# Shifting the weight buffers of an fp32 encoder kernel by steps of 64 bytes in SBUF, and a smaller reserve for DMA descriptors

## The chip, the cores and the metric

The kernel runs on one NeuronCore of a Trainium2 chip (trn2). The metric is the device time of one execution in microseconds; three executions of the kernel before the change are at hand, and one further execution was recorded by the hardware profiler.

A NeuronCore has five engines that run side by side and meet only at semaphores. TensorE (PE) multiplies matrices: a weight load brings a stationary operand of 128 columns into the array, and a matmul then streams a moving operand past it and adds into PSUM. VectorE (DVE) and ScalarE (ACT) work elementwise, GpSimd (POOL) is nearly unused here, and SyncE (SP) issues the DMAs. The on-chip memory SBUF has 128 partitions; a tile of 4 KB here means 4 KB in every partition.

## The reference, cut to what matters

The program is two layers of an encoder on 512 tokens with a model width of 1,024, all in float32.

```
for l in range(DEPTH):                                     # DEPTH = 2
    mod = (cond @ w_ada[l] + b_ada[l])                     # six vectors of 1024
    h = _rmsnorm(x, norm1_w[l]) * (1.0 + sc1) + sh1
    x = x + g1 * _token_mixers(h, w_in[l], ..., w_out[l])  # conv, dilated attention, HGRN2
    h = _rmsnorm(x, norm2_w[l]) * (1.0 + sc2) + sh2
    x = x + g2 * _conv_ffn(h, w_up[l], conv_f_w[l], w_down[l])
return _rmsnorm(x, final_norm_w)
```

The large products are `h @ w_in` (1,024 to 3,584 columns), the mixed heads times `w_out` (1,024 to 1,024), `h @ w_up` (1,024 to 5,632) and the gated result times `w_down` (2,816 to 1,024). Between the first two lie three token mixers; between the last two lies a depthwise convolution of width 3 with a gelu gate.

## The kernel before, in words

**Products in three passes.** TensorE multiplies here in the type fp32r. Because one such product does not carry all the bits of a float32, every operand is held as two parts: a high part, which is the value cast to fp32r, and a low part, which is what the cast left over. A product is then the sum of three: high by high, high weight by low activation, low weight by high activation. The method `block` (lines 399 to 412) issues the three for one 128 by 128 piece of a weight:

```
        self.mm(ps, wh[:, s], ah, first if start is None else start, False)
...
        self.mm(ps, wh[:, s], al, False, False)
...
        self.mm(ps, wl[:, s], ah, False, last)
```

Of three matmuls two load their stationary operand from the high part `wh` of the weight and one from the low part `wl`. `s` is a slice of 128 columns, thus 512 bytes, so every slice of a buffer starts at the same place within 512 bytes as the buffer does. The moving operand is 512 tokens wide in the loop `tile_gemm` (line 712) and 256 wide in `first_group` and `last_group` (lines 683 and 618), which work on halves of the tokens at the seams between the stages.

**The way of a weight.** The weights are cut into chunks of up to 1,024 columns, in the order of their use (`run`, lines 1339 to 1358). `loader` (line 351) issues one DMA on SP for each chunk, into one of three buffers `wr`. `splitter` (line 358) makes the parts: a cast on ACT or DVE writes `wh` from `wr`, and a subtraction on DVE writes `wl` from `wr` and `wh`. There are four buffers `wh0` to `wh3` and four `wl0` to `wl3`, taken in turn: `sb` (line 225) takes the free buffer of a tag that was freed longest ago. Chunks that are marked wide (those of `first_group` and `last_group`) may also use buffers of other tags as weights: `qk`, `PT`, `KK`, `QQ`, `S`, `TT`, `bias`, `wa` and `ap`.

**What sets the order.** The kernel is written as generators. `run_threads` (line 322) advances them by priority and by a model of the engines' clocks (the class `Clock`, line 110) while the program is built, and the order of the instructions on every engine is the order in which they were issued then. The model knows the sizes of the tiles and the costs of operations; it does not look at addresses.

**Where the buffers lie.** `place` (line 218) takes all SBUF buffers once, in the order of the list `ORDER`, before any other tile, so that they lie one behind the other. The list `BUFFERS` gives the size of each in KB and their number:

```
BUFFERS = dict(wr=(4, 3), wh=(4, 4), wl=(4, 4), hx=(4, 8), qk=(4, 2), PT=(4, 4), KK=(4, 1), QQ=(4, 1), S=(4, 1),
               TT=(6, 1), ao=(2, 2), vr=(2, 2), va=(2, 1), bias=(4, 2), wa=(4, 1), tmp=(2, 5), P=(2, 2), sc=(1, 1),
               ap=(4.25, 1), acc=(2, 2), sm=(0.03125, 8), km=(2, 1), gs=(2, 3), qr=(2, 2), t2=(2, 2))
ORDER = ["wh", "wl", "wa", "bias", "wr", "tmp", "km", "P", "ap", "acc", "gs", "qr", "vr", "va", "ao", "t2", "sc",
         "hx", "PT", "TT", "qk", "KK", "QQ", "S", "sm"]
```

The sizes of the buffers ahead of `ap`, and of those from `acc` to `S`, are multiples of 512 bytes; `ap` with 4,352 bytes is eight and a half times 512. So all of `wh`, `wl`, `wa`, `bias`, `wr`, `tmp`, `km`, `P` and `ap` start at the same place within 512 bytes, and all of `acc` to `S`, with the activations `hx` among them, start 256 bytes off that place. Counted in lines of 64 bytes, of which eight make 512, the two groups are four lines apart. Ahead of all of them lies a stretch of SBUF that is reserved for descriptors of DMAs whose descriptors software writes; the keyword `dynamic_dma_scratch_size` of the program's constructor in `kernel` (line 1423) sets its size.

Of the kernel before, what the change touches and what calls it, by code (L numbers as in the profile page):

```python
# [9 lines left out]
F32 = mybir.dt.float32  # L10
# [182 lines left out]
class Kernel:  # L193
# [23 lines left out]

    def place(self):

        for tag in ORDER:  # L220
            for o in self.free_slots[tag]:
                self.one.tile([128, o["size"]], F32, tag=o["name"], name=o["name"] + "_0")


# [1212 lines left out]
```

## Time and profile before

| what | value |
|---|---|
| median of three runs | 1370.9 us (1370.58 to 1371.35) |
| the profiled execution's own time | 1370.76 us |
| its span, first to last instruction | 1369.0 us |
| mean granted clock of TensorE | 0.991 |
| instructions | 24,502 |
| bytes moved by DMA | 169.19 MB, mean 124 GB/s |

The profile records one execution. Its span is 1.76 us shorter than the time of that execution, which also holds what lies before the first and after the last instruction. "PE" are matmuls and "PEld" weight loads, which run ahead of the matmuls and overlap them. A line such as L274 is the line in the code that issues the instruction; L274 is the helper for matmuls and L181 the helper for all operations of DVE and ACT, so groups are told apart by the names of the tiles, output first, then inputs. Buffer numbers are left out of the names. A matmul's recorded duration holds its latency; how fast matmuls follow each other has to be read from their starts.

### The profile page before, as it was taken

The numbers are of one execution on the slowest core, as the hardware profiler recorded it, in microseconds if no ns is written. First come the engines' busy times: TensorE is split into PE (matmuls) and PEld (weight loads), VectorE is DVE, ScalarE is ACT, GpSimd is POOL, SyncE is SP. The second block draws the span as 40 slices with busy tenths as digits, with TensorE's granted clock in tenths as the row PEclk, the third lists the DMA queues.
The fourth block names the chain that finished last, engine by engine and source line by source line (L and its number), as shares of the span: only waits on it lengthen the run. The fifth ranks groups of instructions, "written<-read, shape, count | busy, mean of one in ns | idle before, by whom it ended". The sixth has DMA issues, their size and how long they took to land.

```text
span 1369.0 us, 24502 instructions
## 1 busy us (share of the span) xinstructions
PE 1344.9 (98%) x10042; PEld 1112.4 (81%) x10042; DVE 1070.0 (78%) x1841; ACT 609.6 (45%) x1017; POOL 2.1 (0%) x16
## 2 busy tenths in 40 slices
PE   8999999999999999999999999999999999999997
PEld 7977767778988888888899777777898888888887
DVE  6799999898599999766695999888868565556666
ACT  4537556565342433333453473746535232233332
POOL 0000000000000000000000000000000000000000
PEclk8999999999999999999999999999999999999998
DMA  9534443232348788432431312011422323323221
GB/s 353 189 134 142 124 151 94 81 105 89 103 148 293 254 280 290 126 108 70 140 99 63 106 54 99 32 53 54 139 78 57 128 76 95 101 86 122 77 93 63
DMA packets 55264, 169.19 MB, mean 124 GB/s; under 512 B 6256, under 2 KB 8304, under 8 KB 55152
## 3 DMA queue, kind: packets, MB, share of 16 engines
q1 hardware_dynamic: 55152, 167.63, 37.9%
q8 instruction: 79, 1.29, 0.4%
q14 instruction: 33, 0.27, 0.1%
HBM read 165.50 MB, written 2.10 MB: 122 GB/s over the span
## 4 chain that ended last, share of the span: by engine, by line
PE 84%; DVE 12%; ACT 2%; issue 1%; DMA 0%; SPq 0%; DVEq 0%; ACTq 0%
PE m L274 53%; PE g L274 29%; DVE acc L181 2%; PE m L280 2%; DVE KK L181 2%; DVE QQ L181 1%; DVE wl L181 1%; DVE TT L181 1%; DVE wa L181 1%; DVE P L181 1%; DVE hx L181 1%; DVE x L181 1%; DVE st L181 0%; DVE sc L181 0%; DMA x<-xT 0%
## 5 line engine op out<-in xcount | busy, mean ns | idle before, releaser
L274 PE MATMUL g<-hx,wh 128*128 128x512 f32 (+1 forms) x1288 | 402.6, 390 | 0.9 <-DVE qk L181 0.8
L274 PE MATMUL m<-hx,wh 128*128 128x512 f32 (+1 forms) x1136 | 318.0, 364 | 0.0
L181 DVE TENSOR_TENSOR wl<-wr,wh 128x1024 fp32r<-128x1024 f32 (+3 forms) x215 | 220.5, 1027 | 90.4 <-ACT wh L181 79.4
L274 PEld LDWEIGHTS g<-hx,wh 128*128 128x128 f32 x1288 | 237.2, 189 | 53.2 <-issue 7.7
L181 ACT CAST wh<-wr 128x1024 fp32r<-128x1024 f32 (+3 forms) x176 | 157.1, 893 | 250.9 <-PE m L274 155.0
L274 PE MATMUL g<-hx,wl 128*128 128x512 f32 (+1 forms) x648 | 252.7, 390 | 0.0
L274 PEld LDWEIGHTS m<-hx,wh 128*128 128x128 f32 x1136 | 204.3, 189 | 34.2 <-issue 0.6
L274 PE MATMUL m<-hx,wl 128*128 128x512 f32 (+1 forms) x576 | 209.0, 363 | 0.0
L274 PEld LDWEIGHTS g<-hx,wl 128*128 128x128 f32 x648 | 122.5, 189 | 25.4 <-issue 3.8
L274 PEld LDWEIGHTS m<-hx,wl 128*128 128x128 f32 x576 | 108.7, 189 | 16.9
L181 DVE SCALAR_TENSOR_TENSOR x<-m,mod,x 128x256 f32<-128x256 f32 (+1 forms) x112 | 66.2, 592 | 43.1 <-PE m L274 42.1
L181 DVE SCALAR_TENSOR_TENSOR acc<-ap,par,acc 128x512 f32<-128x512 f32 x120 | 89.8, 748 | 2.2
L181 DVE SCALAR_TENSOR_TENSOR tmp<-m,par,tmp 128x511 f32<-128x511 f32 x120 | 89.1, 746 | 1.9
L181 ACT ACTIVATE P<-P,sm 128x512 f32<-128x512 f32 x72 | 51.5, 721 | 42.6 <-DVE sm L181 42.2
L181 ACT ACT_TABLE_LOAD x49 | 62.9, 1283 | 6.0 <-DVE sm L181 4.5
L181 DVE CAST wh<-wr 128x1024 fp32r<-128x1024 f32 (+3 forms) x41 | 24.5, 598 | 52.4 <-PE m L274 37.1
L181 ACT ACTIVATE tmp<-tmp 128x512 f32<-128x512 f32 x44 | 27.8, 632 | 73.1 <-DVE tmp L181 73.0
L181 ACT COPY km<-KK 128x512 f32<-128x512 f32 x30 | 20.5, 683 | 80.2 <-DVE KK L181 58.8
L181 ACT ACTIVATE tmp<-m,par 128x512 f32<-128x512 f32 x60 | 40.7, 686 | 34.5 <-PE m L274 32.8
L181 DVE CUSTOM_DVE_ANT_0 bias<-bias,cb,par 128x1024 f32<-128x1024 f32 x39 | 49.5, 1278 | 2.3 <-DMA bias<-w_ada 2.3
L181 DVE CUSTOM_DVE_ANT_0 wa<-wa,cb,par 128x1024 f32<-128x1024 f32 x39 | 49.9, 1278 | 0.7 <-DMA wa<-w_ada 0.7
L181 ACT ACTIVATE tmp<-x 128x256 f32<-128x256 f32 (+1 forms) x64 | 28.4, 444 | 46.4 <-DVE x L181 42.4
(319 smaller groups left out, 2158.0 us busy)
## 6 DMA issues: line engine op xcount, KB each, us to landing
wr<-w_up SPq DMA_DIRECT2D x76, 512.0 KB, 3.5
wr<-w_in SPq DMA_DIRECT2D x44, 512.0 KB, 3.5
bias<-w_ada SPq DMA_DIRECT2D x39, 512.0 KB, 4.5
wa<-w_ada SPq DMA_DIRECT2D x39, 512.0 KB, 4.0
wr<-w_down SPq DMA_DIRECT2D x32, 320.0 KB, 2.9
wr<-w_down SPq DMA_DIRECT2D x32, 256.0 KB, 2.6
wr<-w_in SPq DMA_DIRECT2D x16, 384.0 KB, 4.4
wr<-w_up SPq DMA_DIRECT2D x16, 384.0 KB, 3.3
```

The lines of the kernel that those rows point to most:

```text
L181: r = f(*a, **k)
L274: self.nc.tensor.matmul(out, lhsT=lhsT, rhs=rhs, start=start, stop=stop, **kw)
L280: self.nc.tensor.transpose(out, in_, self.ident)
```

## The change

Seven tiles of 16 float32 (64 bytes) are put between the eight buffers of the weights' parts: one ahead of `wh1`, `wh2`, `wh3` and one ahead of each of `wl0` to `wl3`. No instruction reads or writes them. The stretch reserved for DMA descriptors is set to 1,024 bytes per partition, which leaves room for the seven tiles.

```diff
     def place(self):
 
+
         for tag in ORDER:
-            for o in self.free_slots[tag]:
+            for i, o in enumerate(self.free_slots[tag]):
+                if tag in ("wh", "wl") and i + (tag == "wl"):
+                    self.one.tile([128, 16], F32, name=f"line_{o['name']}")
                 self.one.tile([128, o["size"]], F32, tag=o["name"], name=o["name"] + "_0")
...
-    nc = bacc.Bacc("TRN2", target_bir_lowering=False, num_devices=1)
+    nc = bacc.Bacc("TRN2", target_bir_lowering=False, num_devices=1, dynamic_dma_scratch_size=1024)
```

Counted in lines from the start of `wh0`, the buffers `wh0` to `wh3` then begin at lines 0, 1, 2, 3 of eight and `wl0` to `wl3` at lines 4, 5, 6, 7; before, all eight began at line 0. The buffers from `wa` to `ap` move from line 0 to line 7, and those from `acc` to `S` from line 4 to line 3. Among themselves these two groups stay four lines apart.

## The prediction

> **What bounds the kernel now.** I read the page's busy times first, then the chain that ended last.
>
> ```profile
> span 1369.0 us, 24502 instructions
> ...
> PE 1344.9 (98%) x10042; PEld 1112.4 (81%) x10042; DVE 1070.0 (78%) x1841; ACT 609.6 (45%) x1017; POOL 2.1 (0%) x16
> ...
> PE 84%; DVE 12%; ACT 2%; issue 1%; DMA 0%; SPq 0%; DVEq 0%; ACTq 0%
> PE m L274 53%; PE g L274 29%; DVE acc L181 2%; PE m L280 2%; DVE KK L181 2%; DVE QQ L181 1%; DVE wl L181 1%; DVE TT L181 1%; DVE wa L181 1%; DVE P L181 1%; DVE hx L181 1%; DVE x L181 1%; DVE st L181 0%; DVE sc L181 0%; DMA x<-xT 0%
> ```
>
> TensorE is busy for 98% of the span and holds 84% of the chain. VectorE's 12% are spread over many small steps, and the one that touches the shifted buffers, the subtraction that writes wl, has 1% of the span. DMA has 0%. A busy matmul can still be a waiting one, so the next view is the table by stretches, for the two long products of the feed-forward part.
>
> ```profile
> 340.00:660.00 320.00, 320.00 (x1546) 270.59 (x1545) 259.23 (x387) 113.03 (x162) 0.00 (x0) 1.00 0.55 181
> ...
> 1000.00:1320.00 320.00, 320.00 (x1532) 270.12 (x1531) 198.80 (x266) 105.98 (x150) 0.00 (x0) 1.00 0.30 91
> ```
>
> The columns are the stretch, its length, the busy time of PE, PEld, DVE, ACT and POOL with their instructions, the granted clock, the DMA share and GB/s. Over these 640 us TensorE never stops, and its granted clock is full. Only the pace at which matmuls follow each other can move the end there. That pace stands in the chain in order of time (start, length, what) and in the timeline of TensorE (start, busy time, line, operation, tiles and shapes).
>
> ```profile
> 380.04 10.88 PE g L274 x48
> 390.92 23.12 PE m L274 x102
> ```
>
> ```profile
> 680.00 0.52 PE L274 MATMUL m<-TT,qk 128*128 128x256 f32 x3
> 680.36 0.40 PE L274 MATMUL m<-S,wh 128*128 128x256 f32 x2
> 680.60 0.28 PE L274 MATMUL m<-S,wl 128*128 128x256 f32 x1
> ...
> 681.44 0.52 PE L274 MATMUL m<-TT,qk 128*128 128x256 f32 x3
> ```
>
> The first fence gives 48 matmuls of 512 columns in 10.88 us and 102 in 23.12 us, 226.7 ns each. In the second, the rows left out hold six more matmuls, so twelve of 256 columns start between 680.00 and 681.44, 120.0 ns each. The difference, 106.7 ns for 256 columns, is 0.4167 ns a column; what is left is 226.7 - 512 x 0.4167 = 13.3 ns a matmul, at both widths. This fixed part is the only thing in the bound that a shift of a buffer could take away. The Trainium skill, page "TensorE: Matmul & The Clock Gate", section "Back-to-back issue gap", gives a warm matmul N / 2.4 + 2.5 ns, so 215.8 and 109.2 ns at these widths; the trace is 10.9 and 10.8 ns above it, and by the page most of the 13.3 ns would be a stall.
>
> **The change part by part.** First, what it moves. I count in lines of 64 bytes, eight to 512 bytes. Before, wh and wl start at one line and the activations hx (and PT, TT, qk, KK, QQ, S, which take their place later) four lines further: `ap` has 4,352 bytes, 8.5 x 512, and lies between. After it, the distance from a weight buffer to the activations is 3, 2, 1, 0 lines for wh0 to wh3 and 7, 6, 5, 4 for wl0 to wl3. So wh3 comes to distance 0, wl3 keeps distance 4, and the other six get the distances 1, 2, 3, 5, 6 and 7.
>
> Does the distance matter to the pace? Weight load and moving operand do run in step:
>
> ```profile
> 382.37 0.39 PE L274 MATMUL g<-hx,wl 128*128 128x512 f32 x1
> 382.38 0.41 PEld L274 LDWEIGHTS g<-hx,wh 128*128 128x128 f32 x2
> ...
> 382.60 0.61 PE L274 MATMUL g<-hx,wh 128*128 128x512 f32 x2
> ```
>
> The next weight load begins 10 ns after the matmul, to the timeline's grain, so two streams read SBUF from starting lines that the layout fixes, and a collision would come in every matmul alike. But the trace before holds two distances already. In the fence at 680 us the weights in qk lie in the same group as their moving operand TT, at distance 0; the weights of the other rows, wh and wl in those shown and ap, bias and wa in the rows left out, lie four lines from theirs. From 680.00 to 680.36 three matmuls at distance 0 take 120.0 ns each; from 680.36 to 681.44 nine at distance 4 take 120.0 ns each. Nothing separates the two. Two of eight distances are a sample, not a proof, but they are the nearest and the farthest. For the six others I take 0 ns, by these rows, and keep as bounds that the whole 13.3 ns goes, or that it comes a second time.
>
> The Trainium skill, page "SBUF — State Buffer", section "Who interferes with whom", says that only the port pair which VectorE and GpSimd share can collide, and that TensorE's two reading ports, one for the moving operand and one for weight loads, are independent of each other. By that rule no distance can matter and this change is worth nothing; the rows agree for distances 0 and 4, and no row here shows the others.
>
> The price of the bounds needs the number of matmuls:
>
> ```profile
> L274 PE MATMUL g<-hx,wh 128*128 128x512 f32 (+1 forms) x1288 | 402.6, 390 | 0.9 <-DVE qk L181 0.8
> L274 PE MATMUL m<-hx,wh 128*128 128x512 f32 (+1 forms) x1136 | 318.0, 364 | 0.0
> ...
> L274 PE MATMUL g<-hx,wl 128*128 128x512 f32 (+1 forms) x648 | 252.7, 390 | 0.0
> ...
> L274 PE MATMUL m<-hx,wl 128*128 128x512 f32 (+1 forms) x576 | 209.0, 363 | 0.0
> ```
>
> The buffers are taken in turn, so one wh buffer serves (1288 + 1136) / 4 = 606 of these matmuls and one wl buffer (648 + 576) / 4 = 306. At 13.3 ns a matmul that is 8.1 us for a wh buffer and 4.1 us for a wl buffer; the six buffers with new distances make 3 x 606 + 3 x 306 = 2736 matmuls and 36.4 us. The down projection, whose moving operand stands under other names, is left out of these counts, so the prices are floors. By the page's 10.9 ns the 2736 would give 29.8 us.
>
> Second, the cast and the subtraction that fill the buffers. Their operands change distance too: wr goes to line 7, wh to 0 to 3, wl to 4 to 7. Rows of the wide chunks show other distances already:
>
> ```profile
> L181 DVE TENSOR_TENSOR wl<-wr,wh 128x1024 fp32r<-128x1024 f32 x123 | 150.2, 1222 | 74.4 <-ACT wh L181 64.6 <-PE m L274 6.0 <-PE m L280 0.3
> ...
> L181 DVE TENSOR_TENSOR QQ<-wr,S 128x1024 fp32r<-128x1024 f32 x2 | 2.4, 1220 | 0.5 <-ACT S L181 0.5
> ...
> L181 DVE TENSOR_TENSOR TT<-wr,KK 128x1024 fp32r<-128x1024 f32 x1 | 1.2, 1205 | 0.0
> ```
>
> ```profile
> L181 ACT CAST wh<-wr 128x1024 fp32r<-128x1024 f32 x100 | 105.0, 1050 | 146.6 <-PE m L274 96.1 <-PE g L274 36.6 <-DMA wr<-w_up 9.2
> ...
> L181 ACT CAST S<-wr 128x1024 fp32r<-128x1024 f32 x2 | 2.1, 1056 | 1.9 <-DMA wr<-w_down 1.9
> ```
>
> With all three operands at one line the subtraction takes 1222 ns; with the second input and the output four lines off (QQ, TT) 1220 and 1205. The casts take 1050 and 1056. I take zero. The ends are -17 ns of 1222 by the row farthest off, -1.4%, and as much upward, since no row excludes it; the step holds 1% of the chain, rounded, so at most 1.5% of 1369.0 = 20.5 us, and the ends are 0.3 us either way. Where it isn't on the chain, TensorE's work covers it; if that cover were gone, the same 17 ns on the 123 rows would be 2.1 us.
>
> Third, the DMAs. The buffers behind wl move by seven lines, and with them the places that wr, wa, bias and x are loaded to.
>
> ```profile
> 2.59 5.64 DMA x<-xT
> ```
>
> ```profile
> q1 hardware_dynamic: 55152, 167.63, 37.9%
> ...
> wr<-w_up SPq DMA_DIRECT2D x76, 512.0 KB, 3.5
> ```
>
> One DMA wait stands in the longest pieces of the chain, 5.64 us for x at the start. A row of x has 2,048 bytes, 32 lines; if its new start cost or saved one line in 32, that is 0.2 us either way. I take zero. All weights come on SP's hardware queue, landing after 3.5 us.
>
> Fourth, the reserve. It serves descriptors that software writes; the rows show one data queue, of the hardware kind, issued by SP, and POOL busy for 2.1 us in 16 instructions. Nothing uses what is taken away: zero, and no other engine is there to cover it or to need cover.
>
> Fifth, the order. No instruction is added or removed, and the model that orders them does not know addresses. No wait is added, and nothing is queued behind anything new.
>
> The sum against the profiled execution: 1369.0 span + 1.76 around it + 0 = 1370.76 us, 0.1 us under the median of the runs. I state the forecast against the median: 1370.9 us. Its own range from the second and third parts and the spread of the runs is 1370.0 to 1371.8. About 0.2%, 2.7 us, is what a measurement of this kernel can tell from no change.
>
> **The rivals.** The first ends faster: the 13.3 ns are a collision of the two reading streams, and some of the distances 1, 2, 3, 5, 6, 7 avoid it. For it speaks that the fixed part is the same at 256 and 512 columns, that the streams start in step, and that it is larger than the skill's page has it. Against it speaks that distances 0 and 4 give the same 120.0 ns; a collision that depended on the line would have to spare neither. One or two buffers freed give -4.1 to -12.2 us, 1358.7 to 1366.8. All six freed give -36.4 us, 1334.5; all of the page's 10.9 ns would give 1341.1.
>
> The second ends slower: at a distance at which the matmul's stream runs just behind or just ahead of the weight load, the two meet once more, and a matmul pays 13.3 ns again. Its place is TensorE in the two long products, where every ns counts. It decides from the first buffer that is hit: a wl buffer gives 1375.0, a wh buffer 1379.0, all six 1407.3. Against it stand the same two distances; for it, that six were never tried in this trace.
>
> The third is that the change does not do what it says: the tiles between the buffers are placed elsewhere, or all distances stay. It too gives 1370.9 and cannot be told from the forecast by time.
>
> **How the numbers follow.** I give no effect 0.68, the third rival being some 0.03 of it. The faster rival gets 0.18, half for one or two buffers and half for more. The slower one gets 0.14. The range has to take in 0.12 beyond the forecast: the single buffer on the fast side, 4.1 to 8.1 us, reaches down to 1362.8, say 1362, and the single wl buffer on the slow side reaches 1375.0, say 1376. Left out are some 0.2: the larger gains and the larger losses. Faster by over 0.2% is 0.18, within 0.2% is 0.68, slower is 0.14.
>
> **What would show it right or wrong.** Right: in the stretches 340 to 660 and 1000 to 1320 us TensorE is again busy throughout, the chain again has 48 matmuls in 10.88 us, the subtraction stays at 1222 ns within 10, and the order of the instructions is the same. The faster rival would show as runs of 24 or 48 matmuls that take less than 226.7 ns each, for some tiles and not for others in a cycle of four; the slower one as the same with 240 ns. The forecast is wrong if the pace within one tile changes with its buffer, or if the small steps of VectorE in the mixers move by more than 1%.

## The result, and the profile after

The changed kernel takes 1382.03 us (median of four runs, 1380.82 to 1383.94) against 1370.84 us before (median of four, 1370.58 to 1371.35). The ratio is 1.0082 with a 95% interval of 1.0065 to 1.0100: slower by 11.2 us, where no change had been forecast.

The page of the changed kernel, in the parts that answer to those quoted before (the three lines that the change adds in the code move L274 to L277):

```profile
span 1381.3 us, 24502 instructions
...
PE 1357.7 (98%) x10042; PEld 1112.3 (81%) x10042; DVE 1070.6 (78%) x1841; ACT 609.3 (44%) x1017; POOL 2.1 (0%) x16
...
PE 86%; DVE 10%; ACT 2%; issue 1%; DMA 1%; SPq 0%; DVEq 0%; ACTq 0%
PE m L277 54%; PE g L277 30%; PE m L283 2%; DVE wl L181 1%; DVE KK L181 1%; DVE QQ L181 1%; DVE acc L181 1%; DVE wa L181 1%; DVE P L181 1%; DVE TT L181 1%; ACT P L181 1%; DVE x L181 1%; DVE hx L181 1%; DMA x<-xT 0%; ACT tmp L181 0%
```

The instructions are as many as before, the busy times of VectorE and ScalarE within 0.6 us of theirs, and TensorE is busy 12.8 us longer. Its share of the chain rose by two points, at VectorE's cost. The same engine does the same work more slowly, or does it with more waits that count as busy. The chain in order of time (start, length, what) tells where. Of the changed kernel:

```profile
380.37 11.09 PE g L277 x48
391.46 23.61 PE m L277 x102
...
452.53 27.75 PE m L277 x120
...
674.51 34.45 PE m L277 x242
...
1041.86 11.09 PE g L277 x48
...
1336.00 34.44 PE m L277 x242
```

And of the kernel before, the pieces that stand at the same places of the work and were not quoted yet:

```profile
668.57 34.35 PE m L274 x242
...
1035.63 10.88 PE g L274 x48
...
1323.95 34.36 PE m L274 x242
```

Read the starts as marks. The long products of the first layer's feed-forward part begin at 380.04 before and 380.37 after; the last group behind them begins at 668.57 and 674.51. The stretch grew from 288.53 to 294.14 us, by 5.61 us. In the second layer the same stretch runs from 1035.63 to 1323.95 before and from 1041.86 to 1336.00 after, 288.32 and 294.14 us, 5.82 us more. Both together are 11.43 of the 12.3 us by which the two spans differ; everything ahead of the first stretch adds 0.33 us, and what lies between them 0.29 us. Within the stretches the pace changed: 102 matmuls in 23.61 us are 231.5 ns each and 120 in 27.75 us 231.3 ns, where all took 226.7 ns before.

By the tables by stretches TensorE is never idle in these windows and its granted clock is full, as before:

```profile
340.00:660.00 320.00, 320.00 (x1525) 266.51 (x1524) 257.29 (x383) 111.93 (x160) 0.00 (x0) 1.00 0.54 180
1000.00:1320.00 320.00, 320.00 (x1533) 266.84 (x1532) 196.22 (x266) 106.39 (x153) 0.00 (x0) 1.00 0.29 88
```

A busy share of 100% thus looks the same at 226.7 and at 231.3 ns a matmul. The counts of these windows do not show the loss either: they fell from 1546 to 1525 in the first, but in the second there are 1533 where there were 1532, because a window fixed in time holds a different part of the work when the starts move. Only the starts at the same places of the work show it.

The subtraction on VectorE moved by 2 ns at most, whatever lines its operands have now:

```profile
L181 DVE TENSOR_TENSOR wl<-wr,wh 128x1024 fp32r<-128x1024 f32 x123 | 150.2, 1222 | 75.9 <-ACT wh L181 66.7 <-PE m L277 6.0
...
L181 DVE TENSOR_TENSOR QQ<-wr,S 128x1024 fp32r<-128x1024 f32 x2 | 2.4, 1222 | 0.5 <-ACT S L181 0.5
...
L181 DVE TENSOR_TENSOR TT<-wr,KK 128x1024 fp32r<-128x1024 f32 x1 | 1.2, 1207 | 0.0
```

### The profile page after: what moved, and what is told of

Read it like the earlier page. It is cut to its first block, busy times and chain, and to the rows that moved or that the text cites. A ratio compares the mean times of both kernels' runs of the same rounds, so it can differ in the third digit from the quotient of the medians.

```text
span 1381.3 us, 24502 instructions
## 1 busy us (share of the span) xinstructions
PE 1357.7 (98%) x10042; PEld 1112.3 (81%) x10042; DVE 1070.6 (78%) x1841; ACT 609.3 (44%) x1017; POOL 2.1 (0%) x16
## 4 chain that ended last, share of the span: by engine, by line
PE 86%; DVE 10%; ACT 2%; issue 1%; DMA 1%; SPq 0%; DVEq 0%; ACTq 0%
PE m L277 54%; PE g L277 30%; PE m L283 2%; DVE wl L181 1%; DVE KK L181 1%; DVE QQ L181 1%; DVE acc L181 1%; DVE wa L181 1%; DVE P L181 1%; DVE TT L181 1%; ACT P L181 1%; DVE x L181 1%; DVE hx L181 1%; DMA x<-xT 0%; ACT tmp L181 0%
## 5 line engine op out<-in xcount | busy, mean ns | idle before, releaser
L277 PE MATMUL g<-hx,wh 128*128 128x512 f32 (+1 forms) x1288 | 404.6, 391 | 0.8 <-DVE qk L181 0.8
L277 PE MATMUL m<-hx,wh 128*128 128x512 f32 (+1 forms) x1136 | 321.0, 367 | 0.0
L277 PEld LDWEIGHTS g<-hx,wh 128*128 128x128 f32 x1288 | 236.4, 189 | 55.0 <-issue 7.7
L277 PE MATMUL g<-hx,wl 128*128 128x512 f32 (+1 forms) x648 | 253.9, 392 | 0.0
L277 PEld LDWEIGHTS m<-hx,wh 128*128 128x128 f32 x1136 | 204.2, 188 | 37.5 <-issue 0.6
L277 PE MATMUL m<-hx,wl 128*128 128x512 f32 (+1 forms) x576 | 210.8, 366 | 0.0
L277 PEld LDWEIGHTS g<-hx,wl 128*128 128x128 f32 x648 | 122.2, 189 | 27.2 <-issue 3.8
L277 PEld LDWEIGHTS m<-hx,wl 128*128 128x128 f32 x576 | 108.6, 189 | 18.8
```

Of the source, the lines that this page charges most:

```text
L277: self.nc.tensor.matmul(out, lhsT=lhsT, rhs=rhs, start=start, stop=stop, **kw)
```

## The experiments

Distance is counted as in the prediction, from the start of a weight buffer to the moving operand, in lines of 64 bytes. Four questions were open. Is it the smaller reserve? Is it that consecutive weight loads now start on different lines? Is it the distance itself? Or is it other engines' writes into the same lines?

**The smaller reserve alone** (e1_scratch). The edit:

```diff
-    nc = bacc.Bacc("TRN2", target_bir_lowering=False, num_devices=1)
+    nc = bacc.Bacc("TRN2", target_bir_lowering=False, num_devices=1, dynamic_dma_scratch_size=1024)
```

> The smaller reserve alone, all eight buffers on one line again (distance 4 to the activations). Theory D, the distance of weight and moving operand sets the pace: 1370.8 us as before, 226.7 ns a matmul of 512 columns. Theory R, that the reserve or the 15 KB by which every tile then starts lower is what costs: about 1382 us.

It took 1370.88 us against 1370.83 before on the same chip, ratio 0.9999 (0.9990 to 1.0009), and its chain has the old pace, 10.88 / 48 = 226.7 ns:

```profile
378.73 10.88 PE g L274 x48
```

The reserve, and the lower addresses of all tiles, cost nothing. All later kernels that need room have it too.

**All weights at distance 0** (e2_dist0). Instead of the seven tiles, one of 256 bytes ahead of the buffers behind `ap`:

```diff
+                n = {'acc0': 64}.get(o["name"])
+                if n:
+                    self.one.tile([128, n], F32, name=f"line_{o['name']}")
                 self.one.tile([128, o["size"]], F32, tag=o["name"], name=o["name"] + "_0")
```

> All eight buffers on one line, and 256 bytes ahead of the buffers behind ap, so that every weight buffer has distance 0 to the moving operand. Theory M, that consecutive weight loads from different lines cost and one line for all is free whatever its distance: 1370.8 us, 226.7 ns a matmul of 512 columns. Theory D, that each distance has a pace of its own: another pace; the changed kernel's matmuls at distance 0 took 228.7 to 229 ns in the mean where the load after them was at 0 too, which would make 3936 x 2.1 ns = 8 us more, about 1379 us.

1370.66 us, ratio 1.0001 (0.9991 to 1.0010). The pace is 226.7 ns again:

```profile
379.12 10.88 PE g L277 x48
```

So distance 0 is as good as 4 at 512 columns, and the small loss that had been read off the changed kernel's matmuls at distance 0 was not theirs. This left the theory that only unequal lines cost.

**High parts at distance 4, low parts at 0** (e3_two_lines). The same edit with `{'wl0': 64, 'wa0': 64}`.

> wh stays at distance 4, wl goes to distance 0, nothing else moves in relation to the activations. Only the two distances that the kernel before holds occur. Theory D in its simple form (a pace for each distance, added up): one third of the loads at distance 0, two thirds at 4, so a third of the difference that e2_dist0 shows. Theory M: every third pair of loads changes its line, so the pace rises to about 230 ns as in the changed kernel, near 1382 us, even if e2_dist0 stays at 1370.8.

1370.43 us, ratio 0.9996 (0.9987 to 1.0005):

```profile
379.29 10.88 PE g L277 x48
```

Here every third load starts on another line than the one before it, and nothing is lost. The mixture as such is cleared. What was left was that 0 and 4 lines are one case and the distances between them others.

**A map of all distances** (e4_map). A kernel of its own, whose core is:

```
for r in range(REPEAT):                      # 16
    c = 128 * (r % 8)
    h, l = b[:, wh + c:wh + c + 128], b[:, wl + c:wl + c + 128]
    nc.tensor.matmul(p[:, :n], lhsT=h, rhs=b[:, ah:ah + n], start=r == 0, stop=False)
    nc.tensor.matmul(p[:, :n], lhsT=h, rhs=b[:, a2:a2 + n], start=False, stop=False)
    nc.tensor.matmul(p[:, :n], lhsT=l, rhs=b[:, ah:ah + n], start=False, stop=r == REPEAT - 1)
```

> Not the reference's computation: copies x to the output and runs only stretches of 48 matmuls, 16 times high weight by high activation, high weight by low, low weight by high, with the high weight at each of eight distances and the low weight at each of eight, at 512 and then at 256 columns, with no other engine at work. Theory D: the pace follows from the two distances alone, equal in both kernels where both occur: 226.7 ns for (4,4) at 512 and 120.0 ns for (4,4) and (0,0) at 256, and 230 to 232 ns for the pairs of the changed kernel, (0,7), (3,6), (2,5) and (1,4). Theory M: all eight equal pairs 226.7 ns, the 56 unequal ones more. Theory W, that writes of other engines into SBUF collide with TensorE's reads: all 64 pairs the same pace here, 226.7 ns or less.

In the trace the output tile names the stretch: n for 512 columns or h for 256, then the distances of the high and the low weight as letters from a (0) to h (7). The timeline of TensorE shows the first matmul of a stretch and the first of the next one, 48 matmuls later. For (4,4), then the four pairs of the changed kernel, (0,7), (1,4), (2,5) and (3,6):

```profile
420.99 0.39 PE L35 MATMUL nee<-b 128*128 128x512 f32 x1
...
431.88 0.39 PE L35 MATMUL nef<-b 128*128 128x512 f32 x1
...
98.61 0.39 PE L35 MATMUL nah<-b 128*128 128x512 f32 x1
...
109.69 0.39 PE L35 MATMUL nba<-b 128*128 128x512 f32 x1
...
154.07 0.40 PE L35 MATMUL nbe<-b 128*128 128x512 f32 x1
...
165.08 0.39 PE L35 MATMUL nbf<-b 128*128 128x512 f32 x1
...
254.27 0.39 PE L35 MATMUL ncf<-b 128*128 128x512 f32 x1
...
265.47 0.40 PE L35 MATMUL ncg<-b 128*128 128x512 f32 x1
...
354.51 0.39 PE L35 MATMUL ndg<-b 128*128 128x512 f32 x1
...
365.61 0.40 PE L35 MATMUL ndh<-b 128*128 128x512 f32 x1
```

10.89 us for 48 matmuls at (4,4), 11.08 at (0,7), 11.01 at (1,4), 11.20 at (2,5) and 11.10 at (3,6): 226.9, 230.8, 229.4, 233.3 and 231.3 ns. These are the pairs because, as the program is built, the 512-wide chunks take `wh3` with `wl0`, `wh2` with `wl3`, `wh1` with `wl2` and `wh0` with `wl1`. No other engine works in this kernel at that time, so writes of other engines are not the cause. The whole map, as the mean time in ns between the starts of two matmuls of a stretch, with rows for the high weight's distance and columns for the low weight's:

| 512 columns | 0 | 1 | 2 | 3 | 4 | 5 | 6 | 7 |
|---|---|---|---|---|---|---|---|---|
| 0 | 226.7 | 231.3 | 231.0 | 230.9 | 226.9 | 231.2 | 231.0 | 230.9 |
| 1 | 228.9 | 228.9 | 233.7 | 233.5 | 229.4 | 228.9 | 233.7 | 233.5 |
| 2 | 233.3 | 233.2 | 232.4 | 230.2 | 233.2 | 233.2 | 232.4 | 230.2 |
| 3 | 231.2 | 231.7 | 231.1 | 233.4 | 233.3 | 231.8 | 231.1 | 233.4 |

The rows for 4 to 7 repeat those for 0 to 3 within 0.6 ns. The columns repeat the same way, except that the row for 3 has 231.2 at 0 and 233.3 at 4. The map has a period of four lines, 256 bytes: distances 0 and 4 are one point of it, and that point is the best. A further row, with the moving operand and all weights moved together by three lines, gave 226.9, 229.0, 232.4 and 233.4 for equal distances 0 to 3, against 226.7, 228.9, 232.4 and 233.4 on the diagonal: at this width the place itself does not count, the distance does. With both weights at 4 and only the low activation moved by 1, 2 or 3 lines the pace was 232.0, 233.0 and 229.2 ns, so the place of the second pass's moving operand counts too.

At 256 columns the order is another. Pairs of 0 and 4 take 120.0 ns, which only (2,1) and (6,1) reach as well, and the shortest time is 113.6 to 113.8 at (3,1), (3,3) and what equals them modulo four lines. Here a pair does not fix the pace alone: (1,1) took 117.8 ns, and 113.3 with everything moved by three lines. For (3,1), then (4,4):

```profile
1056.99 0.28 PE L35 MATMUL hdb<-b 128*128 128x256 f32 x1
...
1062.45 0.28 PE L35 MATMUL hdc<-b 128*128 128x256 f32 x1
...
1118.61 0.28 PE L35 MATMUL hee<-b 128*128 128x256 f32 x1
...
1124.37 0.28 PE L35 MATMUL hef<-b 128*128 128x256 f32 x1
```

5.46 us for 48 matmuls against 5.76 us.

**One line for all weights, at distance 2** (e5_dist2). If the map holds in the program, a layout without any tile between the buffers must be slow. The edit of e2_dist0 with `{'acc0': 96}`.

> All eight buffers on one line, as before, but 384 bytes ahead of the buffers behind ap, so that every weight has distance 2 to the activations and no two loads start on different lines. Theory P, that the pace is set by the distance modulo 256 bytes, as the map shows it: 232.4 ns in place of 226.7 for 3936 matmuls of 512 columns, +22.4 us, and 118.7 in place of 120.0 for about 1000 of the 1920 matmuls of 256 columns, -1 to -2.5 us; 1390 to 1392 us. Theory M, that unequal lines among consecutive loads are what costs: 1370.8 us.

1386.14 us, ratio 1.0118 (1.0101 to 1.0135). Its chain, with the same marks as above:

```profile
379.61 11.20 PE g L277 x48
...
676.40 34.43 PE m L277 x242
...
1044.47 11.15 PE g L277 x48
...
1340.07 34.47 PE m L277 x242
```

Slower than the changed kernel, with all eight buffers on one line: the distance alone does it. The pace in the stretches, 11.20 / 48 = 233.3 and 11.15 / 48 = 232.3 ns, is that of the map (232.4) within 1 ns. One distance has two paces here: the times between the starts repeat 230, 237, 229, 238, 229, 237 ns in the first layer and a pattern of seven, 230, 232, 241, 232, 231, 232, 228 ns, in the second, and what decides between them is not known. The total was expected 4 to 6 us higher. The stretches grew to 296.79 and 295.60 us, by 8.26 + 7.28 = 15.5 us, nearly all of the 15.9 us by which the span grew. The expectation had counted all 3936 matmuls of 512 columns; the two stretches hold 288.5 / 0.2267 = 1273 each, and at the two paces measured 1273 x 6.6 + 1273 x 5.6 ns = 15.5 us is what came. The others lie around the mixers, where the end hardly moved: the part between the two stretches grew by 1.0 us. How much of their loss other engines' work hid there, and how much the faster 256-wide matmuls gave back, was not separated.

**Finer steps** (e6_fine). The kernel of e4_map with distances in steps of 4 bytes, and with the low activation shifted too.

> Not the reference's computation: x copied to the output, and stretches of 48 matmuls as in e4_map. First all distances of 0 to 252 bytes in steps of 4 bytes, the same for high and low weight, then the high weight, the low weight and the low activation each at 0, 64, 128 and 192 bytes, at 512 and 256 columns. Theory P, steps of whole lines of 64 bytes: flat within a line, 226.7, 228.9, 232.4 and 233.4 ns at 512 columns. Theory F, a smooth dependence on the distance in bytes: values in between, and perhaps a distance below 226.7 ns. At 256 columns some combination near 113.3 ns, as (3,1) had 113.8.

Neither theory has the shape right. For whole lines the paces of e4_map come back, on another chip: 226.7, 229.0, 232.4 and 233.4 ns for 0, 64, 128 and 192 bytes. Between them the pace is neither flat nor smooth: 226.7 ns at 4 bytes, 233.3 at 8, 228.3 at 16, 233.4 at 32, 226.7 again at 136, 243.6 at 100. No distance and none of the 64 mixtures went below 226.7 ns at 512 columns. At 256 columns the lowest of the mixtures were 113.3 to 114.1 ns, for (64, 64, 0), (192, 192, 0) and (192, 64, 0) bytes of high weight, low weight and low activation; of the equal distances 76, 88 and 168 bytes had 113.5. The mixture (192, 64, 0) also stood in e4_map with 113.8. But equal distances of 64 bytes had 117.8 elsewhere in both maps, and equal distances of 192 bytes had 117.8 in the first sweep of this run and 113.6 in its mixtures, at the same addresses: the fast rhythm is not always found.

**Seven tiles of 256 bytes** (e7_pad256). The changed kernel with `[128, 64]` in place of `[128, 16]`.

> The changed kernel with one number changed: the seven tiles between the buffers have 256 bytes in place of 64. Theory P, that only the distance modulo 256 bytes counts: no distance changes, 226.7 ns at 512 columns, 1370.8 us. Any theory by which the tiles between the buffers, or their seven different steps as such, cost: about 1382 us.

1370.33 us against 1371.2 us, ratio 0.9993 (0.9984 to 1.0003):

```profile
379.24 10.88 PE g L277 x48
```

With the step set to the period, the whole effect of the change is gone.

**A layout for the seams** (e8_seams). The maps point to a version that should beat both kernels: distance 0 for the 512-wide matmuls, and 192 and 64 bytes for the chunks marked wide, whose matmuls have 256 columns. The buffers of `wh`, `wl`, `qk`, `PT`, `KK`, `QQ`, `S`, `bias` and `wa` become 4.25 KB, which leaves their starts where they are modulo 256 bytes, and the splitter places the parts:

```diff
-            hi = self.sb([128, 1024], ["wh"] + more, F32R)[:, :t.shape[1]]
+            oh, ol = (16, 48) if i in self.wide else (0, 0)
+            hi = self.sb([128, 1088], ["wh"] + more, F32R)[:, oh:oh + t.shape[1]]
...
-            lo = self.sb([128, 1024], ["wl"] + more, F32R)[:, :t.shape[1]]
+            lo = self.sb([128, 1088], ["wl"] + more, F32R)[:, ol:ol + t.shape[1]]
```

> All buffers start modulo 256 bytes as in the kernel before, so the 3936 matmuls of 512 columns keep 226.7 ns. Only the chunks marked wide, whose matmuls have 256 columns, are written 64 bytes (high part) and 192 bytes (low part) into their buffers, which are 256 bytes longer for it, so that their distances are 192 and 64 bytes. Theory P: 113.8 to 114.1 ns in place of 120.0, as the maps have it for (3,1): 1920 x 6 = 11.5 us less if all of them are bound by TensorE, about 10 us less without those of the start, 1359 to 1362 us. If other engines' work spoils the rhythm so that those matmuls take 117 to 118 ns: 1366 us. If the distance doesn't matter at 256 columns in the full program: 1370.8 us.

1359.52 us against 1371.2 us on the same chip, ratio 0.9917 (0.9904 to 0.9930): faster by 11.7 us than the kernel before, and 22.5 us under the changed one. The timeline of its last group in the first layer answers to the fence at 680 us in the prediction:

```profile
675.53 0.50 PE L274 MATMUL m<-TT,qk 128*128 128x256 f32 x3
675.87 0.39 PE L274 MATMUL m<-S,wh 128*128 128x256 f32 x2
676.09 0.28 PE L274 MATMUL m<-S,wl 128*128 128x256 f32 x1
...
676.89 0.50 PE L274 MATMUL m<-TT,qk 128*128 128x256 f32 x3
```

Twelve matmuls in 1.36 us are 113.3 ns each, where they took 120.0. The 512-wide ones kept 226.7 ns, as its chain shows:

```profile
375.43 10.88 PE g L274 x48
...
664.11 33.22 PE m L274 x242
...
1025.66 10.88 PE g L274 x48
...
1313.98 21.79 PE m L274 x144
```

The two long stretches took 288.68 and 288.32 us, against 288.53 and 288.32 before. The 11.3 us by which the span shrank against the kernel before lie outside them, where the 256-wide matmuls are: 4.61 us ahead of the first, 5.51 between the two and 1.33 behind the second. The first of these is the least certain, since that stretch began at 378.73 in e1_scratch, 1.31 us earlier than before, with no change in time.

## Why the prediction was wrong

The step that failed stands in the first of "The change part by part": "For the six others I take 0 ns, by these rows". It rested on two distances, called the nearest and the farthest of eight. They were neither: the pace repeats after 256 bytes, so 0 and 4 lines are the same point, and the 256-wide matmuls there were one sample taken twice. With the shifted buffers the 512-wide ones in the two long products took some 231.3 ns instead of 226.7. The runs that show it are e2_dist0, e3_two_lines and e7_pad256, all without effect, against e5_dist2. The sample was also read at 256 columns and carried over to 512, where the loss was; the map ranks the distances differently at the two widths: (3,3) has 233.4 ns at 512, among the slowest, and 113.6 at 256, among the fastest.

The slower rival had the right place (TensorE in the two long products), the right circumstance (distances that the trace before does not hold) and a wrong price. It took one further 13.3 ns for each matmul that is hit. What came is 2.7 to 6.5 ns by pair on the map, in the mean of the four pairs (230.9 + 229.4 + 233.2 + 231.1) / 4 - 226.7 = 4.45 ns. On the 2546 matmuls of the two stretches that makes 11.3 us, and 11.43 were measured there. Pair by pair the program is nearer to even than the map: the chunks of 24 matmuls that follow 380.44 us take 231.2, 231.1, 232.2 and 230.7 ns each in turn, so it is the mean that carries over. Its account by single buffers failed as well: wh3 and wl3 have the good distances 0 and 4, but a pace belongs to the pair of distances in one chunk; wh3 goes with wl0 and wl3 with wh2, and all four pairs of the changed kernel are slow. Its count mixed the widths too: of its 1288 and 1136 matmuls only 1184 and 864 have 512 columns.

The faster rival was right in that the fixed 13.3 ns is no constant: at 256 columns 120.0 fell to 113.3 ns, of 13.3 ns about half. The changed kernel had little of this: only about a third of its 256-wide matmuls have their weights in wh or wl, and the other buffers kept distance 0 or 4. No gain showed in its total. At 512 columns no distance tried took anything off the 13.3 ns. The 215.8 and 109.2 ns from the Trainium skill's formula ("TensorE: Matmul & The Clock Gate", "Back-to-back issue gap"), which that section gives for an isolated matmul, were not reached at either width; the lowest seen are 226.7 and 113.3.

The rule from the Trainium skill's page "SBUF — State Buffer", section "Who interferes with whom", that TensorE's two reading ports are independent, had supported the 0 ns. By it no distance could matter; e4_map, with TensorE alone at work, shows that the distance between what the two read does, and the measurement decides.

The other steps held. Every engine's instructions come in the same order, the subtraction's 1222 ns stayed, the reserve was worth nothing (e1_scratch), and the first long stretch began only 0.33 us later.

What stays open is the mechanism inside TensorE and SBUF. That the pace depends on the distance between weight and moving operand, and that steps of 256 bytes do not change it at 512 columns, is shown. It is not shown why one distance can have two paces (e5_dist2, and 256 columns in both maps). That the two streams collide in SBUF is only argued; the jagged values at steps of 4 bytes fit no simple picture of lines or banks.

## What to carry to other kernels

Where a stretch is bound by back-to-back matmuls, read the pace from the starts of equal pieces in the chain, not from busy shares, and treat the distance between weight and moving buffers modulo 256 bytes as a parameter: measure it in a small map at the widths in use, lay the buffers out, and read the pace again in the full program, because one distance can have two paces. Two samples that agree are worth little before the period of the thing sampled is known. A pad between buffers that merely looks harmless can cost 0.8%, and the right offset, here at 256 columns, gained as much.

## What the runs showed of the hardware that was not expected

With a weight load for each fp32r matmul and all weights at one distance, the time between matmuls of 512 columns is 226.7 to 227.3 ns at 0 or 256 bytes and 228.9 to 233.4 ns at the other whole lines, up to 243.6 ns at 100 bytes. At 256 columns the same good distance is the worst of the whole lines at 120.0 ns, and 192 bytes for the high part with 64 for the low part gives 113.3 to 114.1 ns. For equal whole-line distances at 512 columns the values came back on a second chip to 0.1 ns, and in the full program with the other engines at work 226.7 ns at distance 0 and, within 1 ns, the 232.4 ns at distance 2.
